# First-pass token blocks in pairs of tiles throughout, their low parts in the ring of the projection's weights

## The chip, the cores and the metric

One Trainium2 chip, one core, one launch. The metric is the device time of the whole program in microseconds (us). The kernel before was run three times: 3278.14, 3278.9 and 3288.34 us, median 3278.9.

## The reference, cut to what matters

One layer of a sequence model over 17 tiles of 128 tokens: tile 16 is the prompt (128 context tokens), tiles 0 to 15 are 2048 latent tokens. Only the first steps of the layer bear on the change:

```
h    = rmsnorm(x, norm_mix) * (1 + sc1) + sh1
proj = h @ w_in                       # 1024 -> 3088 columns
u, z_s5, qkv, z_gdn, beta, a = split(proj)
```

`u` (the first 512 columns) feeds a state-space scan over all tokens (S5), `qkv` a chunked delta-rule scan; `beta` and `a` (the last 16 columns) are its gates. An output projection, a gated residual and an MLP follow.

## The kernel before, in words

All products are made in pairs of parts: a value is split into a high part (rounded to the type that TensorE multiplies at one pass) and a low part (the rest), and a product is `wh*H + wl*H + wh*L`. So each 128x128 weight block costs three matmuls for each of the eight 128-row slices of the 1024 inputs: 24 matmuls for 128 output columns.

**First pass** (`first_cols` L258, `first_pass` L290). It goes over blocks of tiles listed in `UBLOCKS` (L221). For each tile `norm_rows` (L249) loads x, adds the position embedding (two PE products, L214 and L211, and VectorE adds, L216) and normalises the rows; `to_cols` (L162) transposes the tile in eight PE transposes (L169), applies scale and shift on VectorE (L176) and writes the high part `uH` on ScalarE (L178) and the low part `uL`, half on VectorE and half on GpSimd (L179). Both are stored to `s_hH` and `s_hL` for later groups (L280). Then for a block of n columns come four channel tiles of 24 matmuls each (L307), whose results ScalarE copies out as `eu` (L311) and SyncE stores to `s_u` (L312), and 16 narrow matmuls for the gates (L316, L318). The inputs of the next block are recorded ahead of the matmuls of this one (L296). Blocks of tiles 16 and 0 to 3 lie in one wide buffer `g0H`, `g0L` that stays for the projection; the others take `uH`, `uL` from a ring of two. Tiles 4, 5, 6 and 7 are blocks of one tile, so 128 columns wide; 8 to 15 go in pairs, 256 columns wide.

**Tables.** With the first `EARLY` blocks (L220) run the four table steps of the S5 scan (`s5_tables` L1193): products on VectorE and GpSimd (`CA`, L1028 to L1033), copies on ScalarE (L1227, L1235), small PE work (L1226, L1249), stores to `s_stab` and a last VectorE step `KK` (L1255). They share one `CA` and one `WI` buffer, so one step follows another.

**Projection of group 0** (`group_proj` L471). After the early blocks, tiles 16 and 0 to 3 are projected for channel tiles 8 to 19 (24 matmuls of 388 and 24 of 258 columns each, L482), alternating with the remaining first-pass blocks. Each of these channel tiles loads raw weights, splits them into `wh` on ScalarE (L414) and `wl` on GpSimd (L415), and stores both to `s_wc` (L398). The two parts come from pool `pw`, with two buffers of 4 KB per partition each. Later groups load `wh` and `wl` back from `s_wc` (L403): 68 times.

**What sets the order.** The program is recorded in loops that alternate generators (L1741 to L1756: three steps of the first pass and one of the tables a time); a scheduler with a timeline model then fixes the order on each engine, before the run. Engines work through their lists in order and wait on semaphores; a buffer is given out again when all who used its tile are done.

Of the kernel before, what the change touches and what calls it, by code (L numbers as in the profile page):

```python
# [9 lines left out]
FR = mybir.dt.float32r  # L10
# [150 lines left out]

def to_cols(k, h, H, L, c0, kind, r):  # L162

    nc = k.nc
    for q in range(2):
# [5 lines left out]
        for a in range(4):  # L171
# [4 lines left out]
            nc.vector.tensor_scalar(raw[:, a], pv[:, a], k.mcol[:, kind, r, i:i + 1], k.mcol[:, kind + 1, r, i:i + 1], op0=OP.mult, op1=OP.add)  # L176
        hv = H[:, 4 * q:4 * q + 4, c0:c0 + 128]
        nc.scalar.activation(hv, raw, AF.Copy)  # L178
        (nc.gpsimd if q in k.lpool and kind == 0 else nc.vector).tensor_tensor(L[:, 4 * q:4 * q + 4, c0:c0 + 128], raw, hv.bitcast(F32), op=OP.subtract)  # L179

# [36 lines left out]
    return x  # L217


EARLY = 6  # L220
UBLOCKS = ((16, 0, 1), (2, 3), (4,), (5,), (6,), (7,), (8, 9), (10, 11), (12, 13), (14, 15))  # L221


def place(t):

    if t == 16:
        return 0, 1
    return (0, 130 + 128 * t) if t < 4 else (t // 4, 1 + 128 * (t % 4))
# [20 lines left out]
def norm_rows(k, t):  # L249

    x = load_x(k, t)
    h = k.px.tile([128, 1024], F32, name="hrow")
    rs = rms_rows(k, k.psm, x, h)
    k.nc.scalar.activation(h, x, AF.Copy, scale=rs)
    return h


def first_cols(k, tiles, early):  # L258


    nc, S = k.nc, k.S
    if tiles[0] == 16 or tiles[-1] < 4:
        H, L = k.g0x
        c0s = [place(t)[1] for t in tiles]
    else:
        H = k.ph.tile([128, 8, 128 * len(tiles)], FR, name="uH")
        L = k.ph.tile([128, 8, 128 * len(tiles)], FR, name="uL")
        c0s = [128 * i for i in range(len(tiles))]
    for c, t in zip(c0s, tiles):
        h = early.pop(t) if t in early else norm_rows(k, t)  # L270
        to_cols(k, h, H, L, c, 0, int(t == 16))
    segs = [(c0s[i], t, m) for (i, t, m) in runs(tiles)]
    for part, X, X0 in (("hH", H, k.g0x[0]), ("hL", L, k.g0x[1])):
        if tiles[0] == 4:

            nc.scalar.activation(X0[:, :, 642:643], X[:, :, 0:1].bitcast(F32), AF.Copy)
        X = X.bitcast(F32)
        for (c, t, m) in segs:
            g, c0 = place(t)
            nc.sync.dma_start(S[f'{part}{g}'][:, :, c0:c0 + 128 * m], X[:, :, c:c + 128 * m])  # L280

            if t + m in (4, 8, 12):
                e = c + 128 * m
                nc.sync.dma_start(S[f'{part}{g + 1}'][:, :, 0:1], X[:, :, e - 1:e])
            if t in (8, 12):
                nc.sync.dma_start(S[f'{part}{g - 1}'][:, :, 513:514], X[:, :, c:c + 1])
    return H, L, segs


def first_pass(k, early):  # L290

    nc, S = k.nc, k.S
    cols = None
    for bi, tiles in enumerate(UBLOCKS):
        H, L, segs = cols or first_cols(k, tiles, early)

        cols = first_cols(k, UBLOCKS[bi + 1], early) if bi + 1 not in (EARLY, len(UBLOCKS)) else None
        yield None
# [93 lines left out]
def load_w(k, ct):  # L392

    nc = k.nc
    if ct not in k.wdone:
        wh, wl = split_w(k, k.I['w_in'][0][:, ct * 128:ct * 128 + 128])
        for i, w in enumerate((wh, wl)):
            nc.sync.dma_start(k.S['wc'][ct, i], w.bitcast(F32).rearrange("p k c->p (k c)"))  # L398
        k.wdone.add(ct)
        return wh, wl  # L400
    ws = [k.pw.tile([128, 8, 128], FR, name=n) for n in ("wh", "wl")]
    for i, w in enumerate(ws):
        nc.sync.dma_start(w.bitcast(F32).rearrange("p k c->p (k c)"), k.S['wc'][ct, i])  # L403
    return ws


def split_w(k, src, p=None, nm=""):
    nc = k.nc
    p = p or k.pw
    wh = p.tile([128, 8, 128], FR, name="wh" + nm)  # L410
    wl = p.tile([128, 8, 128], FR, name="wl" + nm, bufs=1 if nm else k.wlb)
    w = k.pwr.tile([128, 8, 128], F32, name="wraw")
    nc.sync.dma_start(w, src.rearrange("(k p) c->p k c", p=128))
    nc.scalar.activation(wh, w, AF.Copy)  # L414
    nc.gpsimd.tensor_tensor(wl, w, wh.bitcast(F32), op=OP.subtract)  # L415
    return wh, wl
# [1265 lines left out]
def program(tc, I, O):  # L1682
    nc = tc.nc
    k = Ctx()
# [3 lines left out]
    k.ahead = 0  # L1688
    k.acols = ()
    k.lpool = (1,)  # L1690
    k.wlb = 2
    with ExitStack() as top:
        dram = top.enter_context(tc.tile_pool(name="dram", bufs=1, space=bass.MemoryType.DRAM))
        k.S = {n: dram.tile(list(s), F32, name="s_" + n) for n, s in SHAPES.items()}
# [1 line left out]
        def pool(st, n, b, **kw):  # L1696
            return st.enter_context(tc.tile_pool(name=n, bufs=b, reuse_waits="tile", **kw))
# [4 lines left out]
        with ExitStack() as st0:  # L1702
# [12 lines left out]
            with ExitStack() as st:  # L1715
                k.psA = pool(st, "psA", 3, space=PSUM, side="right")
                for n, b in (("pa", 1), ("px", 4), ("psm", 1)):
                    setattr(k, n, pool(st, n, b, side="right"))
                k.pwr = pool(st, "pwr0", 1, side="right")
                k.peu = pool(st, "pe0", 2, side="right")  # L1720
                setup_first(k)
                params(k)
                tabs = ExitStack()
                k.psS = pool(tabs, "psS", 2, space=PSUM)
                for n in ("sa", "sb", "st"):
                    setattr(k, n, pool(tabs, n, 1))
                early = {t: norm_rows(k, t) for t in UBLOCKS[0]}
                with ExitStack() as sm:
                    k.pm = k.pmw = pool(sm, "pmw0", 5, side="right")
                    k.psM, k.mp = k.psA, "gA"  # L1730
                    m0 = modulation(k, 0)
                    advance(m0, 4)
                    s5_setup(k)
                    drain(m0)
                ab_weights(k)
                k.puw = pool(st, "puw", 1, side="right")
                u_weights(k)
                k.ph = pool(st, "ph0", 2, side="right")
                k.psu = k.psd
                first = first_pass(k, early)  # L1740
                tab = seq(*[s5_tables(k, bt) for bt in range(4)])  # L1741

                for _ in range(3 * EARLY):
                    next(first)
                    advance(tab, 1)
                drain(tab)
                tabs.close()
                k.pwr = pool(sg, "pwr1", 2)
                k.pe, k.pew = pool(sg, "pe1", 2), 388
                k.ph = pool(st, "ph0b", 2, side="right")  # L1750
                k.psu = pool(st, "psu", 2, space=PSUM, side="right")
                H, L = ([t[:, q] for q in range(8)] for t in k.g0x)
                k.cur = (H, L, [(0, 388, 385, [(0, 128, 2048), (129, 256, 0)]), (385, 258, 256, [(0, 256, 256)])], 1)
                group = group_proj(k, 0, range(8, 20))

                for i, _ in enumerate(first):  # L1756
                    advance(group, 1)
# [55 lines left out]
            with ExitStack() as st:  # L1813
# [20 lines left out]
                n = 0  # L1834
# [73 lines left out]
```

## Time and profile before

| | us |
|---|---|
| Median of three runs | 3278.9 |
| Profiled execution, its own time | 3283.95 |
| Its span | 3282.2 |
| PE busy, whole span | 3018.0 (92%) |
| DVE / POOL / ACT busy | 1986.4 / 1351.0 / 1113.0 |
| Tiles 4 to 7 (blocks of one tile) and the last tables | about 140 to 240 |
| Group 0 and the blocks of two tiles | about 240 to 405 |
| Scans, later groups | about 405 to 1620 |

PE is the array's matmul stream, PEld its weight loads (they overlap it), DVE VectorE, ACT ScalarE, POOL GpSimd, SP SyncE, which issues the DMAs. An interval written `x8` in the timeline is eight merged instructions. PEclk is the granted clock of TensorE as a share of 2.4 GHz; 0.50 is the lower of its two levels, 1.2 GHz. The DMA share is the mean busy share of 16 DMA engines; issue rows can lie a little beside the traffic they cause, so a short window can show more than 1.00.

### The profile page before, as it was taken

Reading aid. Unit: us, or ns where it says so; the run is one execution under the profiler, and the core shown is the slowest. Engines: PE = TensorE matmul, PEld = TensorE weight load, DVE = VectorE, ACT = ScalarE, POOL = GpSimd, SP = SyncE. Lnnn points to the kernel's source line nnn. Section 1 sums busy time; section 2 is a strip of 40 time slices with the busy share of each in tenths; the row PEclk is TensorE's granted clock in tenths of the full one; section 3 lists DMA queues with packets and bytes.
Section 4 is the critical chain, followed back from the end, with each engine's and each line's share of the span. In section 5 each row is a group of like instructions: output and inputs, shape, how many; then the busy total and the mean of one; then the engine's idle time right before and its main releaser. Section 6 shows DMA issues by size and latency. Waiting matters only on the chain. (4 is left out here: it accounts for less than half of the span.)

```text
span 3282.2 us, 48952 instructions
## 1 busy us (share of the span) xinstructions
PE 3018.0 (92%) x17978; PEld 2554.5 (78%) x17978; DVE 1986.4 (61%) x3842; ACT 1113.0 (34%) x2338; POOL 1351.0 (41%) x983
## 2 busy tenths in 40 slices
PE   5899989889887889988999999999999999999998
PEld 2778967677776677877888778898888887888886
DVE  6635579777776886346545368543358643684445
ACT  2334334424433222234423243322233322433332
POOL 3532223413444332246543454333444544554542
PEclk7889989898988899989999999999999999999999
DMA  7789888966567888899533455322444534553332
GB/s 208 174 178 223 237 292 259 303 220 205 176 223 228 259 277 287 299 301 321 163 95 112 150 164 167 103 77 75 134 123 143 156 97 125 164 170 100 97 96 71
DMA packets 572752, 594.98 MB, mean 181 GB/s; under 512 B 167228, under 2 KB 428592, under 8 KB 569440
## 3 DMA queue, kind: packets, MB, share of 16 engines
q1 hardware_dynamic: 572512, 591.86, 58.9%
q8 instruction: 141, 2.31, 0.3%
q14 instruction: 99, 0.81, 0.1%
HBM read 449.61 MB, written 142.13 MB: 180 GB/s over the span
## 5 line engine op out<-in xcount | busy, mean ns | idle before, releaser
L1411 POOL TENSOR_TENSOR wol<-woraw,woh 128x512 fp32r<-128x512 f32 x320 | 426.7, 1345 | 648.4 <-ACT woh L1410 637.2
L1410 ACT ACTIVATE woh<-woraw 128x512 fp32r<-128x512 f32 x320 | 193.4, 626 | 802.8 <-PE gA L1556 470.8
L1561 DVE TENSOR_TENSOR acc<-acc,gA 128x512 f32<-128x512 f32 x510 | 341.0, 682 | 192.5 <-PE gA L1556 192.4
L1556 PE MATMUL gA<-woh,ffH 128*128 128x512 f32 x1088 | 426.0, 392 | 6.8 <-ACT r L1538 3.9
L1556 PE MATMUL gA<-woh,ffL 128*128 128x512 f32 x1088 | 425.5, 391 | 1.8 <-DVE ffL L1542 1.8
L1556 PE MATMUL gA<-wol,ffH 128*128 128x512 f32 x1088 | 425.0, 391 | 0.0
L1411 POOL TENSOR_TENSOR wil<-wiraw,wih 128x1024 fp32r<-128x1024 f32 x128 | 328.6, 2569 | 112.0 <-PE gA L1534 84.7
L1541 DVE TENSOR_TENSOR r<-r 128x512 f32<-128x512 f32 (+1 forms) x160 | 163.9, 1031 | 304.7 <-ACT ffH L1540 304.4
L1534 PE MATMUL gA<-htH,wih 128*128 128x512 f32 (+1 forms) x1280 | 276.6, 362 | 5.8 <-DVE acc L1561 3.3
L1534 PE MATMUL gA<-htL,wih 128*128 128x512 f32 (+1 forms) x1280 | 272.8, 358 | 0.0
L1534 PE MATMUL gA<-htH,wil 128*128 128x512 f32 (+1 forms) x1280 | 271.9, 357 | 0.0
L1534 PEld LDWEIGHTS gA<-htH,wih 128*128 128x128 f32 x1280 | 222.8, 190 | 39.1 <-DVE acc L1561 5.0
L1534 PEld LDWEIGHTS gA<-htL,wih 128*128 128x128 f32 x1280 | 221.5, 188 | 30.6
L1556 PEld LDWEIGHTS gA<-woh,ffH 128*128 128x128 f32 x1088 | 205.4, 189 | 51.2 <-ACT r L1538 4.8
L1534 PEld LDWEIGHTS gA<-htH,wil 128*128 128x128 f32 x1280 | 220.5, 188 | 29.8
L1556 PEld LDWEIGHTS gA<-woh,ffL 128*128 128x128 f32 x1088 | 205.3, 189 | 44.0 <-DVE ffL L1542 2.2
L1556 PEld LDWEIGHTS gA<-wol,ffH 128*128 128x128 f32 x1088 | 205.3, 189 | 43.0
L482 PE MATMUL d<-hH,wh 128*128 128x258 f32 (+2 forms) x960 | 178.8, 329 | 23.1 <-DMA wh<-s_wc 18.2
L482 PE MATMUL d<-hL,wh 128*128 128x258 f32 (+2 forms) x960 | 177.8, 319 | 9.5 <-DMA hL<-s_hL 9.4
L482 PEld LDWEIGHTS d<-hH,wh 128*128 128x128 f32 x960 | 150.8, 209 | 40.6 <-issue 24.2
L482 PE MATMUL d<-hH,wl 128*128 128x258 f32 (+2 forms) x960 | 176.0, 320 | 0.0
L1410 ACT ACTIVATE wih<-wiraw 128x1024 fp32r<-128x1024 f32 x128 | 134.7, 1052 | 121.1 <-PE gA L1534 80.7
(419 smaller groups left out, 5603.0 us busy)
## 6 DMA issues: line engine op xcount, KB each, us to landing
wiraw<-in_w_mlp_in SPq DMA_DIRECT2D x128, 512.0 KB
woraw<-in_w_mlp_out SPq DMA_DIRECT2D x256, 256.0 KB
wh<-s_wc SPq DMA_DIRECT2D x68, 512.0 KB
wl<-s_wc SPq DMA_DIRECT2D x68, 512.0 KB
wada<-in_w_ada SPq DMA_DIRECT2D x24, 1024.0 KB
KVr<-s_kv SPq DMA_DIRECT2D x34, 512.0 KB
Qr<-s_qkv SPq DMA_DIRECT2D x32, 512.0 KB
woraw<-in_w_out SPq DMA_DIRECT2D x64, 256.0 KB
```

Source lines behind the costliest of these rows:

```text
L482: nc.tensor.matmul(ps[:, 0:w], W_[:, kk, :], X_[kk][:, f:f + w], start=(n == 0), stop=(n == 23))
L1410: nc.scalar.activation(h[:, i:i + n], w, AF.Copy)
L1411: sub.tensor_tensor(l[:, i:i + n], w, h[:, i:i + n].bitcast(F32), op=OP.subtract)
L1534: nc.tensor.matmul(ps[b][:, 0:w], W[:, kk, :], X[:, kk, b * w:b * w + w], start=(m == 0), stop=(m == 23))
L1541: nc.vector.tensor_tensor(r[:, 0:w], r[:, 0:w], r[:, 0:w], op=OP.mult)
L1556: nc.tensor.matmul(ps, X[:, s], W[:, hf], start=(m == 0), stop=(m == 3 * FB - 1))
L1561: nc.vector.tensor_tensor(accs[i][:, c], accs[i][:, c], ps, op=OP.add)
```

## The change

Two things. Tiles 4 to 15 all go through the first pass in pairs (five blocks, up to tile 9, stand beside the tables instead of six blocks up to tile 7). The low part of an early block no longer has a buffer of its own: it is a tile of pool `pw`, whose `wh` and `wl` become one tile `w` of two parts in a ring of two.

```
-EARLY = 6
-UBLOCKS = ((16, 0, 1), (2, 3), (4,), (5,), (6,), (7,), (8, 9), (10, 11), (12, 13), (14, 15))
+EARLY = 5
+UBLOCKS = ((16, 0, 1), (2, 3), (4, 5), (6, 7), (8, 9), (10, 11), (12, 13), (14, 15))
...
-        H = k.ph.tile([128, 8, 128 * len(tiles)], FR, name="uH")
-        L = k.ph.tile([128, 8, 128 * len(tiles)], FR, name="uL")
+        H, L = (k.uparts(n) for n in ("uH", "uL"))
...
-    ws = [k.pw.tile([128, 8, 128], FR, name=n) for n in ("wh", "wl")]
+    ws = two_parts(k)
...
+def two_parts(k):
+
+    w = k.pw.tile([128, 2, 8, 128], FR, name="w")
+    return w[:, 0], w[:, 1]
...
+                ph0 = pool(st, "ph0", 2, side="right")
+
+                k.uparts = lambda n: (ph0.tile([128, 8, 256], FR, name=n) if n == "uH" else
+                                      k.pw.tile([128, 2, 8, 128], FR, name="w").rearrange("p a k c->p (a k c)").rearrange("p (k c)->p k c", c=256))
...
+                ph0b = pool(st, "ph0b", 2, side="right")
+                k.uparts = lambda n: ph0b.tile([128, 8, 256], FR, name=n)
```

On PE, the last early block before is tile 7 alone; these are its last rows, and the first of group 0 (d are result banks, the numbered wh and wl the resident weights of the four channel tiles, uH and uL the block):

```order
L307 MATMUL d<-uH,wh_551 128x128 x8
L307 MATMUL d<-uL,wh_551 128x128 x8
L307 MATMUL d<-uH,wl_552 128x128 x8
L316 MATMUL d<-uH,ab_517 32x128 x8
L318 MATMUL d<-uL,ab_518 32x128 x8
L169 MATMUL gA<-ident,hrow 128x128 x8
L214 MATMUL gA<-posr,ident 64x512 x2
L324 MATMUL d<-ident,abT 128x32
L482 MATMUL d<-g0H,wh 128x388 x8
```

The same place on PE now (line numbers are those of the changed kernel), where the last early block is tiles 8 and 9 and its low part is a tile w:

```order
L306 MATMUL d<-uH,wh_551 128x256 x8
L306 MATMUL d<-w,wh_551 128x256 x8
L306 MATMUL d<-uH,wl_552 128x256 x8
L315 MATMUL d<-uH,ab_517 32x256 x8
L317 MATMUL d<-w,ab_518 32x256 x8
L169 MATMUL gA<-ident,hrow 128x128 x8
L214 MATMUL gA<-posr,ident 64x512 x2
L323 MATMUL d<-ident,abT 128x32 x2
L211 MATMUL gA<-cst_142,ident 128x512
L488 MATMUL d<-g0H,w 128x388 x16
```

There are as many matmuls in a block as before, each over twice the columns, and two blocks fewer in all: 960 L307 matmuls become 768. Tiles 8 and 9 have moved ahead of group 0.

On SP, the loads of stored weights in a later group, before (wh and wl are single tiles with their buffer numbers, s_wc the stored weights):

```order
L403 DMA wl_4877<-s_wc_61 128x1024
L403 DMA wh_4876<-s_wc_61 128x1024
L514 DMA s_qkv_70<-ec3_4477 128x2x128
L133 DMA wada_4434<-in_w_ada 128x2048
...
L403 DMA wl_5095<-s_wc_61 128x1024
L403 DMA wh_5094<-s_wc_61 128x1024
```

The same place on SP now:

```order
L402 DMA w_4293<-s_wc_61 128x1024 x2
L520 DMA s_qkv_70<-ec3_3646 128x128
L520 DMA s_qkv_70<-ec3_3646 128x2x128
L520 DMA s_qkv_70<-ec3_3683 128x2x128
L133 DMA wada_4144<-in_w_ada 128x2048
...
L402 DMA w_4520<-s_wc_61 128x1024 x2
```

Before, wl often stood ahead of wh, since its buffer came free first; now both parts wait for one tile and go high part first.

On PE, the end of group 0 now, where before all of it stood ahead of the first scan product (L1294, now L1300; ub and WI are the scan's inputs):

```order
L1300 MATMUL gs<-ub,WI 64x272 x4
L488 MATMUL d<-g0H,w 128x388 x16
L488 MATMUL d<-g0L,w 128x388 x3
L1300 MATMUL gs<-ub,WI 64x272 x4
L488 MATMUL d<-g0L,w 128x388 x5
```

The first-pass generator has three steps fewer after the early blocks, so three channel tiles of group 0 are left over for the loop that runs them beside the scan.

## Rows read from the trace of the kernel before

**Rows 1.** The page: busy us, share of the span, instructions

```profile
PE 3018.0 (92%) x17978; PEld 2554.5 (78%) x17978; DVE 1986.4 (61%) x3842; ACT 1113.0 (34%) x2338; POOL 1351.0 (41%) x983
```

**Rows 2.** Stretches: length, busy PE, PEld, DVE, ACT, POOL, PEclk, DMA share, GB/s

```profile
140.00:240.00 100.00, 91.85 (x691) 79.75 (x691) 36.77 (x77) 36.72 (x77) 44.38 (x33) 0.76 0.84 167
...
260.00:400.00 140.00, 136.33 (x971) 126.98 (x970) 67.69 (x147) 54.75 (x102) 35.41 (x47) 1.00 0.87 223
400.00:460.00 60.00, 45.53 (x306) 37.53 (x305) 53.80 (x162) 13.04 (x33) 10.42 (x11) 0.86 0.95 347
```

**Rows 3.** Busy time by stretches, first-pass matmuls of L307 alone

```profile
140.00:240.00 100.00, 59.17 (x384) 0.76 0.84 167
260.00:400.00 140.00, 48.51 (x376) 1.00 0.87 223
```

**Rows 4.** Timeline of PE, tile 7 alone (start, length, merged instructions)

```profile
219.93 1.11 PE L307 MATMUL d<-uH,wh 128*128 128x128 f32 x8
220.88 1.06 PE L307 MATMUL d<-uL,wh 128*128 128x128 f32 x8
```

**Rows 5.** Timeline of PE, a block of two tiles

```profile
343.97 1.12 PE L307 MATMUL d<-uH,wh 128*128 128x256 f32 x8
344.92 1.12 PE L307 MATMUL d<-uL,wh 128*128 128x256 f32 x8
```

**Rows 6.** Timeline of PE at the lower clock, 128 and 258 columns

```profile
154.80 1.91 PE L307 MATMUL d<-uL,wh 128*128 128x128 f32 x8
156.51 1.91 PE L307 MATMUL d<-uH,wl 128*128 128x128 f32 x8
...
435.79 1.92 PE L482 MATMUL d<-hH,wl 128*128 128x258 f32 x8
437.51 1.92 PE L482 MATMUL d<-hL,wh 128*128 128x258 f32 x8
```

**Rows 7.** Groups by line, gate matmuls in 140:245, then in 260:400

```profile
L316 PE MATMUL d<-uH,ab 128*32 128x128 f32 x32 | 3.0, 243 | 0.8 <-ACT eu L311 0.8
...
L316 PE MATMUL d<-uH,ab 128*32 128x256 f32 x32 | 4.4, 280 | 0.0
```

**Rows 8.** Timeline, end of the last table and start of group 0

```profile
180.47 0.17 DVE L1255 TENSOR_TENSOR KK<-KK,gs 128x16 f32<-128x16 f32 x1 [0.91 <-ACT KK L1254]
...
211.58 0.16 DVE L1255 TENSOR_TENSOR KK<-KK,gs 128x16 f32<-128x16 f32 x1
...
240.87 1.70 PE L482 MATMUL d<-g0H,wh 128*128 128x388 f32 x8
```

**Rows 9.** Timeline of PE, transposes and position products of one tile

```profile
252.89 1.03 PE L169 MATMUL gA<-ident,hrow 128*128 128x128 f32 x8
253.85 1.07 PE L214 MATMUL gA<-posr,ident 32*64 32x512 f32 x4
...
257.46 1.02 PE L211 MATMUL gA<-cst,ident 128*128 128x512 f32 x2
```

**Rows 10.** DMA queue (packets, MB, share of 16 engines): 140:260, 280:320, 440:480; issues

```profile
q1 hardware_dynamic: 44117, 21.05, 82.8%
...
q1 hardware_dynamic: 15189, 8.41, 93.4%
...
q1 hardware_dynamic: 3976, 8.70, 65.2%
...
s_u<-eu SPq DMA_DIRECT2D x16, 64.0 KB
s_hL<-uL SPq DMA_DIRECT2D x4, 512.0 KB
```

**Rows 11.** Waits in 140:245 (total us, times, longest)

```profile
POOL CA L1028 <- ACT WI L1235: 15.7, 2, 9.5
```

**Rows 12.** Waits of PE in 400:1780, and the issues of line 403

```profile
PE d L482 <- DMA wh<-s_wc: 18.2, 10, 7.7
L403 SPq DMA_DIRECT2D wl<-s_wc x68: 319/389/1875, 410.5 to 1412.3; - x68
```

More of the change, by code (lines that the diff above doesn't have):

```diff
@@ L404, in load_w @@
     return ws
+def two_parts(k):
+    w = k.pw.tile([128, 2, 8, 128], FR, name="w")
+    return w[:, 0], w[:, 1]
 def split_w(k, src, p=None, nm=""):
     nc = k.nc
-    p = p or k.pw
-    wh = p.tile([128, 8, 128], FR, name="wh" + nm)
-    wl = p.tile([128, 8, 128], FR, name="wl" + nm, bufs=1 if nm else k.wlb)
+    if p is None:
+        wh, wl = two_parts(k)
+    else:
+        wh, wl = (p.tile([128, 8, 128], FR, name=n + nm, bufs=1) for n in ("wh", "wl"))
     w = k.pwr.tile([128, 8, 128], F32, name="wraw")
@@ L1690, in program @@
     k.lpool = (1,)
-    k.wlb = 2
     with ExitStack() as top:
@@ L1737, in program @@
                 u_weights(k)
-                k.ph = pool(st, "ph0", 2, side="right")
+                ph0 = pool(st, "ph0", 2, side="right")
+                k.uparts = lambda n: (ph0.tile([128, 8, 256], FR, name=n) if n == "uH" else
+                                      k.pw.tile([128, 2, 8, 128], FR, name="w").rearrange("p a k c->p (a k c)").rearrange("p (k c)->p k c", c=256))
                 k.psu = k.psd
@@ L1749, in program @@
                 k.pe, k.pew = pool(sg, "pe1", 2), 388
-                k.ph = pool(st, "ph0b", 2, side="right")
+                ph0b = pool(st, "ph0b", 2, side="right")
+                k.uparts = lambda n: ph0b.tile([128, 8, 256], FR, name=n)
                 k.psu = pool(st, "psu", 2, space=PSUM, side="right")
```

## The prediction

> **What bounds the kernel now.** I read the page first, then the busy time by stretches, then the timeline of PE in the stretch that the change touches, then the waits and the DMA queue. On the page the reader sees PE busy 92% of the span [rows 1]: time taken from PE counts wherever PE is what the others wait for. The stretches say where that is. In 140 to 240, where tiles 4 to 7 go through the first pass one by one, PE is busy 91.85 of 100 us, at a mean granted clock of 0.76 of full; DVE, ACT and POOL are each under 45. In 260 to 400, with pairs and group 0, PE is busy 136.33 of 140 at full clock. Between 400 and 460 PE idles 14.5 of 60 us and DVE is the busiest, so what comes there depends on the scan [rows 2]. So the touched stretch is bound by PE, with the tables and the DMA (share 0.84) close behind, and the stretch after it passes any shift on.
>
> **What a block costs.** The first-pass matmuls alone show the reason for the change: 384 of them took 59.17 us for four tiles, and 376 took 48.51 us for nearly eight [rows 3]. In the timeline, groups of eight matmuls follow each other every 0.89 us over 128 columns and every 0.95 us over 256, both at full clock [rows 4, 5]. At the lower clock it is 1.71 us over 128 and 1.72 us over 258 [rows 6]. So a matmul of half the columns costs as much: 111 ns against 119, or 214 against 215.
>
> The Trainium skill (TensorE: Matmul & The Clock Gate, "Back-to-back issue gap") speaks against this in one table: 134 cycles for 128 columns and 262 for 256, warm and isolated. By it alone two pair blocks would cost what four single ones do, and the sum would be 0. The same section says that a stream of weight loads and matmuls is paced by both, so that narrow ones take longer than the table; the rows side with that sentence. I keep the table as a rival.
>
> **The sum on PE.** Removed: the four single blocks, 59.17 us [rows 3], and their gate matmuls, 3.0 us for L316 and as much taken for L318 [rows 7]: 65.2. Added: two pair blocks of 12 groups of eight, and gate matmuls of 4.4 us per four blocks and line [rows 7], so 4.4 for two blocks and both lines.
> - At full clock: 24 x 0.95 + 4.4 = 27.2, saving 38.
> - At the lower clock throughout: 24 x 1.72 = 41.3, and gates 4.4 x 1.72/0.95 = 8.0, saving 16.
> - At the clock that the stretch has now: 59.17/48 = 1.23 us per group means that (1.23 - 0.89)/(1.71 - 0.89), or 0.42 of the groups, ran low. Then a pair's group takes 0.58 x 0.95 + 0.42 x 1.72 = 1.27 us; 24 of them and gates of 5.9 make 36.4, saving 29.
>
> Nothing in the change raises the clock for certain, so PE by itself would give 29.
>
> **What comes next in line.** When PE is lighter, two other chains can end last.
>
> The tables: their last KK step ends at 211.58, 31 us after that of the table before (180.47) [rows 8]. Their steps share one buffer each, and POOL waited up to 9.5 us for ACT to free one [rows 11], so I leave their end where it is. In the new order the block of tiles 8 and 9 stands behind the last table's matmuls, with the transposes and position products of one or two tiles, about 1.0 us each and three per tile [rows 9]. The block takes 12 x 0.95 + 2.2 = 13.6 at full clock or 12 x 1.27 + 3.0 = 18.2 at the mixed one. Group 0 then starts between 211.6 + 3 + 13.6 = 228 and 211.6 + 6 + 18.2 = 236. Now it starts at 240.87 [rows 8] with tiles 8 and 9 still to do, worth 13.6 + 6 = 19.6, so the comparable moment is 260.5. Gain 24 to 32.
>
> The DMA: 82.8% of 120 us is 99.4 us of work in 140 to 260. Two stretches give the price of a packet: 15189 packets and 8.41 MB took 93.4% of 40 us on 16 engines (598 us), 3976 packets and 8.70 MB took 65.2% (417 us), so about 17 ns each beside 40 us per MB, an estimate from these two rows. The bytes stay, but 16 stores of u become eight of twice the run, 1024 runs each, and four stores each of uH and uL become two [rows 10]: 8 x 1024 + 4 x 1024 = 12288 fewer packets, 13 us of the share. That leaves 86 us; at the 93.4% that the rows reach it needs 92 us of the 120, so 28 is the most it lets through.
>
> The least of the three is at the low end of the tables' range; I take 25, near it because the clock is mixed.
>
> **Edits that I cost at nothing.**
> - Low parts in the ring of weights. Tile (4, 5) and (8, 9) share a buffer, (6, 7) has the other, so the first weights of group 0 may be split while the block (8, 9) runs, the second ones only when its matmuls and its store are done. That wait is on ACT, ahead of the last copies of `eu`, for which PE's next result banks wait. The nearest row is POOL's 9.5 us behind ACT [rows 11]; the store is issued a block earlier, so I take 0 and keep 0 to 9.5.
> - `wh` and `wl` in one tile. The low part's reload, once ahead, now waits for the last eight matmuls of its channel tile, under 1 us, while the high part no longer queues behind it. PE waited 18.2 us in all, 10 times, for the high part, in 68 loads [rows 12]. I take 0; the price is in the rivals.
> - Three channel tiles of group 0 beside the scan. They could fill part of the 14.5 idle us after 400 [rows 2], or push the scan's first copies back; between -14 and +14, taken as 0.
> - The later lists change in their interleaving only: no matmul is added or taken there.
>
> Sum: the profiled execution's own 3283.95 (span 3282.2 and 1.75 around it) - 25 = 3258.95. The median of the runs is 5.05 below the profiled one, so 3254.
>
> **Rivals.**
> - The tables or the transfers pace the early stretch (0.20). For it: DMA share 0.84 and tables ending only 29 us before group 0 [rows 2, 8]; pairs need the inputs of two tiles before their first matmul, so each table step may slip behind a longer norm chain. If each of the two last steps slips by the 9.5 us seen [rows 11], 25 - 19 = 6 is left: 3273. Against: POOL and DVE are busy under 45 of 100 us there.
> - The merged weight tile makes PE wait in later groups (0.08). Place: the start of each channel tile, L482 and its 68 loads. Price: eight matmuls, 0.95 us, for each load that now comes late. From 26 late loads on it eats the gain; if half of them, 34, and the 10 waits that exist grow by as much again, it is about 42 us: 3283.95 - 25 + 42 - 5.05 = 3296. Against: 58 of 68 loads show no wait.
> - The later stretch is dealt out anew by the scheduler and comes out some 20 us better or worse (0.08): 3234 to 3274, or beyond with a smaller gain. The idle 14.5 us in 400 to 460 show that there is something to win and lose.
> - Cost goes by columns (0.02): a pair's matmul would take twice a single's, two blocks the 65.2 us of four, and the time stays at 3279. Equal spacing at either width nearly excludes it [rows 4 to 6]. It is what the table of the Trainium skill cited above would give.
>
> **How the numbers follow.** Forecast 0.62, with its own range 3242 to 3266 (savings of 13 to 37, from the low-clock to the full-clock sum). About 0.3% (9.8 us) is what a measurement of this kernel can tell from no change. Faster: 0.62, a fifth of the first rival (0.04) and half of the third (0.04), 0.70. Slower: the second, 0.08, and a quarter of the third, 0.02, 0.10. The rest, 0.20, is no change. The range of 8 in 10 reaches from 3238 to 3278: it takes in the first rival and leaves out the second, the far ends of the third and a little of the forecast's best case.
>
> **What would show it.** Right: 256-column groups of eight every 0.95 us for tiles 4 to 7, those matmuls together some 30 us instead of 59; the first matmul of group 0 by 228 to 236 with tiles 8 and 9 done, and the end of group 0 about 25 us earlier; later stretches shifted as they are. Wrong: PE waiting longer for uH or uL or for ACT's `eu` copies in 140 to 240 with tables that end after 215; a sum of waits for s_wc well above 18 us; or a shift at 400 that is gone by 1600.

## The result, and the profile after

The changed kernel took 3244.62 us (median; 3242.63 to 3258.06) against 3283.04 us of the kernel before in the same comparison (3278.14 to 3288.34): 0.9891 of it, 95% interval 0.9858 to 0.9925. In a later comparison it was 3249.46 against 3280.29, 0.9904 (0.9886 to 0.9921). So it gained 38 and 31 us, where 25 were forecast, and it lies inside the forecast's own range. The profiled execution took 3243.24 us, its span 3241.4, 40.8 us less than the span before. How these 40.8 us are made up is another matter: the forecast put them all ahead of group 0's end, and only a part of them lies there.

The page of the changed kernel (busy us, share, instructions) answers to [rows 1]; 31.3 us less PE, nearly nothing elsewhere:

```profile
PE 2986.7 (92%) x17754; PEld 2521.9 (78%) x17754; DVE 1991.4 (61%) x3840; ACT 1112.6 (34%) x2326; POOL 1353.5 (42%) x983
```

The stretches of [rows 2] in the changed kernel (length, busy PE, PEld, DVE, ACT, POOL, granted clock, DMA share, GB/s), and in the second fence its first-pass matmuls alone (L306 now; busy PE and PEld only), as in [rows 3]:

```profile
140.00:240.00 100.00, 85.05 (x707) 70.16 (x706) 48.01 (x110) 47.99 (x89) 47.50 (x38) 0.91 0.88 224
260.00:400.00 140.00, 125.65 (x852) 116.37 (x854) 76.22 (x171) 48.80 (x93) 31.53 (x44) 0.95 0.90 262
400.00:460.00 60.00, 55.30 (x392) 44.10 (x384) 53.74 (x168) 25.80 (x78) 21.02 (x17) 0.99 0.79 266
```

```profile
140.00:240.00 100.00, 37.48 (x288) 36.23 (x288) 0.91 0.88 224
260.00:400.00 140.00, 27.18 (x216) 26.00 (x214) 0.95 0.90 262
```

In the first stretch TensorE runs at a mean clock of 0.91 instead of 0.76 and does 288 double-width matmuls in 37.48 us, where 384 single-width ones took 59.17. But in 260 to 400, which was full (136.33 of 140 at clock 1.00), PE now idles 14.4 us instead of 3.7, and its clock is 0.95. 8.8 of these 14.4 us are two waits, at 386 and at 395, for copies of projection results; the scan, which now starts at 364, has its first steps there (the first of the two waits is shown below). In 400 to 460 it is the other way: 4.7 us idle instead of 14.5.

The timeline of the changed kernel where group 0 starts, PE first, then ACT, then the last step of the tables on DVE (start, length, instructions, in brackets the idle time before and what ended it); these answer to [rows 5] and [rows 8]:

```profile
185.38 1.12 PE L306 MATMUL d<-w,wh 128*128 128x256 f32 x8
...
206.51 4.24 PE L306 MATMUL d<-uH,wh 128*128 128x256 f32 x21 [1.37 <-ACT uH L178]
...
230.42 4.60 PE L488 MATMUL d<-g0H,w 128*128 128x388 f32 x16 [5.60 <-ACT eu L310]
...
221.69 0.38 ACT L319 ACTIVATE abT<-d 32x256 f32<-32x256 f32 x1 [4.82 <-PE d L317]
226.63 1.06 ACT L420 ACTIVATE w<-wraw 128x1024 fp32r<-128x1024 f32 x1 [4.57 <-DMA x<-in_x_sample]
229.99 0.38 ACT L310 ACTIVATE eu<-d 128x256 f32<-128x256 f32 x1 [2.30 <-DMA s_u<-eu]
...
200.72 0.17 DVE L1261 TENSOR_TENSOR KK<-KK,gs 128x16 f32<-128x16 f32 x1
```

Groups of eight over 256 columns take what they took in [rows 5], every 0.95 us where they run at full clock, as forecast. Group 0 starts at 230.42, inside the forecast 228 to 236, but not by the forecast's terms: the tables end 11 us earlier than before (200.72, not 211.58), the block of tiles 8 and 9 runs from 206.5 to 221.6, and then PE waits 5.60 us for ACT. On ACT the split of the next channel tile's weights (L420) stands ahead of a copy of `eu` (L310); ACT idles 4.57 us before the split, and another 2.30 before the copy.

The end of group 0 is not the same event in the two kernels, since scan products now stand inside it. What can be compared is the moment at which two of its channel tiles are left, the blocks of the first pass are done and no scan product has run. (Three are left over in the order in which the program is recorded; on PE two stand behind the first scan product.) On PE, before and then after:

```profile
390.60 1.57 PE L482 MATMUL d<-g0H,wh 128*128 128x388 f32 x8
...
405.38 1.86 PE L1294 MATMUL gs<-ub,WI 128*64 128x272 f32 x12
```

```profile
363.98 1.14 PE L1300 MATMUL gs<-ub,WI 128*64 128x272 f32 x8
365.05 3.09 PE L488 MATMUL d<-g0H,w 128*128 128x388 f32 x16
...
386.00 3.78 PE L488 MATMUL d<-g0H,w 128*128 128x258 f32 x16 [4.60 <-DVE ec L512]
389.57 1.66 PE L488 MATMUL d<-g0L,w 128*128 128x258 f32 x8
```

That moment came at 363.98 instead of 390.60, 26.6 us earlier, and at 369.17 in the repeat of the changed kernel, 21.4 earlier. The two channel tiles that were left took 14.6 us before and 26.9 now, 12.3 more. 5.6 of these are 36 scan products, which before stood behind group 0 (PE by groups in 355 to 391):

```profile
L1300 PE MATMUL gs<-ub,WI 128*64 128x272 f32 x32 | 4.5, 405 | 0.0
L1368 PE MATMUL gs<-ub,WT 128*128 128x272 f32 x4 | 1.1, 392 | 0.0
```

4.6 are the wait at 386.00, for a copy on DVE that stands behind the first steps of the scan (L1318), which themselves waited for the scan's products:

```profile
379.87 0.63 DVE L1318 TENSOR_TENSOR Tt<-S,tb 128x272 f32<-128x272 f32 x1 [11.54 <-ACT S L1304]
...
385.24 0.61 DVE L512 SCALAR_TENSOR_TENSOR ec<-d,cw,ec 128x385 f32<-128x385 f32 x1
```

The remaining 2 us are the last matmuls, at a lower clock behind the wait: 3.78 us for 16 of 258 columns, where the tile before took 2.07.

To see where all the time went, I cut both executions at two events: the last projection matmul of group 0, and the first matmul of the output projection. Before, then after, columns as in the stretches above:

```profile
140.00:405.20 265.20, 252.80 (x1818) 229.22 (x1818) 123.77 (x267) 101.95 (x199) 85.73 (x84) 0.91 0.86 205
405.20:1438.70 1033.50, 893.35 (x7046) 754.49 (x7044) 750.10 (x1942) 353.29 (x981) 337.92 (x302) 0.91 0.78 255
1438.70:3282.20 1843.50, 1782.94 (x8588) 1513.22 (x8588) 1013.24 (x1378) 612.30 (x1085) 866.89 (x549) 0.98 0.44 136
```

```profile
140.00:390.90 250.90, 225.76 (x1671) 199.30 (x1670) 129.07 (x287) 102.54 (x190) 85.17 (x86) 0.95 0.91 243
390.90:1390.80 999.90, 887.65 (x7010) 753.26 (x7009) 755.47 (x1918) 350.54 (x973) 341.05 (x299) 0.91 0.79 256
1390.80:3241.40 1850.60, 1783.36 (x8588) 1512.93 (x8588) 1007.90 (x1378) 612.96 (x1085) 864.16 (x549) 0.98 0.44 135
```

- Early (140 to the end of group 0): 14.3 us less, with the 36 scan products (5.6 us) now inside. PE's busy time fell by 27.0, its idle time rose from 12.4 to 25.1; the waits of 5.60 and 4.60 us shown above are most of that rise.
- Middle (scans and later groups): 33.6 us less, with 36 matmuls fewer (x7046, x7010), the scan products above. For the same work it is 28.
- Late: 7.1 us more, with the same 8588 matmuls; idle 60.6 before, 67.2 after.

The forecast had 25, 0 and 0. The idle time of the middle fell by 28 us. Among PE's waits there (400 to 1440), the ones for DMA fell from 43.2 us in all to 15.1. The wait for stored weights of [rows 12] nearly went (total, times, longest):

```profile
PE d L488 <- DMA w<-s_wc: 0.4, 1, 0.4
```

Three explanations of the middle stood to be tested: the merged weights' tile (its 18.2 us of waits became 0.4), the scan that now starts inside group 0 (364 instead of 405), and a third, called theory C: the change has no part of its own in it, and the middle's length depends on how the scheduler happens to deal out the same work, by idle time and by time at the low clock.

### The profile page after: what moved, and what is told of

It reads as the page before. It is cut to its first block, busy times and chain, and to the rows that moved or that the text cites. A ratio compares the mean times of both kernels' runs of the same rounds, so it can differ in the third digit from the quotient of the medians.

```text
span 3241.4 us, 48395 instructions
## 1 busy us (share of the span) xinstructions
PE 2986.7 (92%) x17754; PEld 2521.9 (78%) x17754; DVE 1991.4 (61%) x3840; ACT 1112.6 (34%) x2326; POOL 1353.5 (42%) x983
## 2 busy tenths in 40 slices
DMA packets 560270, 594.96 MB, mean 184 GB/s; under 512 B 158844, under 2 KB 416112, under 8 KB 556960
## 5 line engine op out<-in xcount | busy, mean ns | idle before, releaser
L488 PE MATMUL d<-hH,w 128*128 128x258 f32 (+2 forms) x1920 | 335.8, 322 | 7.5 <-ACT ec L508 4.2
L488 PEld LDWEIGHTS d<-hH,w 128*128 128x128 f32 x1920 | 289.4, 203 | 34.8 <-issue 20.5
L488 PE MATMUL d<-hL,w 128*128 128x258 f32 (+2 forms) x960 | 180.8, 321 | 7.4 <-DMA hL<-s_hL 7.1
L1548 DVE TENSOR_TENSOR ffL<-r,ffH 128x512 fp32r<-128x512 f32 (+1 forms) x160 | 169.8, 1069 | 1.8
```

The costliest lines, as they stand in the source:

```text
L488: nc.tensor.matmul(ps[:, 0:w], W_[:, kk, :], X_[kk][:, f:f + w], start=(n == 0), stop=(n == 23))
L1548: nc.vector.tensor_tensor(fL[:, bs], r[:, 0:w], fH[:, bs].bitcast(F32), op=OP.subtract)
```

## The experiments

All ratios are to the kernel before, measured in the same comparison, with 95% intervals; a time is the median, a stage comes from the one profiled execution.

**Does the merged tile do it?** The kernel before with `wh` and `wl` merged into one tile, and nothing else.

```
-    ws = [k.pw.tile([128, 8, 128], FR, name=n) for n in ("wh", "wl")]
+    ws = two_parts(k)
...
+        wh, wl = two_parts(k)
```

> The kernel before with one edit: wh and wl of a channel tile lie in one tile of two parts; blocks and low parts as before. Theory A (the merged tile puts the load of the high part first and so ends PE's waits for stored weights in the later groups): the waits of PE for s_wc, 18 us before, fall under 3 us, and the time is 10 to 20 us under the kernel before. Theory B (the middle gained because three channel tiles of group 0 run beside the scan): waits may change, but the time stays within 6 us of before. Theory C (the middle's 28 us are luck of the scheduler): any shift between -15 and +15, without the waits for s_wc as its main part.

3318.21 us, 1.0112 (1.0059 to 1.0166): 35 us slower. The middle of this run, and then PE's wait for stored weights (total, times, longest):

```profile
406.60:1476.00 1069.40, 931.68 (x7047) 779.37 (x7045) 755.87 (x1942) 356.58 (x981) 346.56 (x303) 0.88 0.76 246
```

```profile
PE d L489 <- DMA w<-s_wc: 10.5, 3, 7.6
```

The wait for weights fell from 18.2 to 10.5 us, and the middle still became 35.9 us longer. Its idle time is that of before (137.7 against 140.1): what grew is the busy time of the same 7047 matmuls, by 38 us, at a clock of 0.88 instead of 0.91. So the merged tile alone is no gain, and fewer waits for stored weights did not make the middle shorter.

**The pairs without the merged tile.** The changed kernel with `wh` and `wl` in rings of their own; the low part of an early block is split into halves that lie in the two rings, and each half has stores of its own.

```
-    ws = two_parts(k)
+    ws = [k.pw.tile([128, 8, 128], FR, name=n) for n in ("wh", "wl")]
...
+class Halves:
+    def __init__(self, k):
+        self.h = [k.pw.tile([128, 4, 256], FR, name=n) for n in ("wh", "wl")]
```

> The changed kernel, but wh and wl keep their own rings of two; the low part of an early block is two halves, one in a buffer of each ring (two stores instead of one). Pairs and the order of the first pass stay. Theory A: the 20 us at the end of group 0 stay, and some 18 us of waits for stored weights come back: about 3262. Theory B: the time stays within 6 us of the changed kernel, 3245.

3278.72 us, 0.9986 (0.9964 to 1.0009): no difference to before that can be told. Its middle:

```profile
399.90:1436.80 1036.90, 905.30 (x7010) 766.70 (x7009) 762.87 (x1919) 351.69 (x973) 345.81 (x300) 0.89 0.76 247
```

The early stretch (259.9) keeps 5 us of its 14, and the first scan product comes at 373.11, 17.5 us ahead of the comparable moment before, not 26.6; the middle's 34 us are gone. Set the four kernels beside each other by their middle: single tiles and two rings 1033, single tiles and a merged tile 1069, pairs and two rings 1037, pairs and a merged tile 1000. The merged tile costs 36 us with single tiles and gains 37 with pairs; the whole times agree (35 longer, 34 shorter). But the two kernels with pairs also start the scan inside group 0 (x7010) and the two with single tiles do not, so the pairs are not the only difference between the columns. A part of a change whose effect turns its sign with another part is no term that one can add up.

**Is it the width?** The changed kernel with the channel products of tiles (4, 5) and (6, 7) done as two runs of 128 columns.

```
+            cols_ = [(0, 128), (128, 256)] if 4 <= tiles[0] < 8 else [(0, n)]
+            for (a, b) in cols_:
...
-                    nc.tensor.matmul(ps[:, 0:n], W_[:, kk, :], X_[:, kk, f:f + n], start=(m == 0), stop=(m == 23))
+                        nc.tensor.matmul(ps[:, a:b], W_[:, kk, :], X_[:, kk, f + a:f + b], start=(m == 0), stop=(m == 23))
```

> The changed kernel, with the u products of the early pairs (4,5) and (6,7) issued as two runs of 128 columns each; inputs, copies, stores and the block (8,9) stay in pairs. If the width of the matmuls is what the first 400 us gained: 192 matmuls more, 12 groups of eight at 0.89 to 1.71 us each pair, so 21 us later at full clock and up to 40 at the lower one: 3265 to 3285, and the gain at the start of group 0 is gone. If stores in fewer runs and fewer waits for the eu buffers gained it: within 8 us of the changed kernel.

3277.65 us, 0.9977 (0.9952 to 1.0002). Narrow groups of this run (L309) at the low clock and at full clock, the end of its tables, the start of its group 0, and in a fence of their own its two stages:

```profile
177.14 1.91 PE L309 MATMUL d<-uH,wl 128*128 128x128 f32 x8
...
213.43 1.05 PE L309 MATMUL d<-uH,wh 128*128 128x128 f32 x8
...
240.80 0.17 DVE L1264 TENSOR_TENSOR KK<-KK,gs 128x16 f32<-128x16 f32 x1 [0.91 <-ACT KK L1263]
...
255.55 4.67 PE L491 MATMUL d<-g0H,w 128*128 128x388 f32 x16 [3.99 <-ACT w L423]
```

```profile
140.00:419.30 279.30, 260.61 (x1883) 234.74 (x1883) 135.21 (x287) 105.68 (x196) 87.94 (x88) 0.91 0.82 219
419.30:1434.50 1015.20, 892.19 (x7011) 759.08 (x7009) 759.38 (x1920) 351.52 (x973) 340.08 (x300) 0.90 0.77 252
```

Group 0 starts 25 us later than in the changed kernel and the early stretch is 28 us longer: the width of the matmuls is what the early stretch gains from. And the tables, which the forecast took to have a pace of their own, end 40 us later (240.80 against 200.72) with no change in their own work. So they have no pace of their own. Their small matmuls stand in PE's line, which is the likely link; no run takes it apart.

**Is it the earlier scan?** The changed kernel with the rest of group 0 drained before the scan is recorded.

```
-            for _ in group:
-                scans.go()
+            drain(group)
```

> The changed kernel, but the three channel tiles of group 0 that are left over are finished before the first step of the scan, as in the kernel before. Theory B (the earlier scan makes the gain of the middle): the first scan product moves from 364 to after the end of group 0 (about 392), and the time rises by 15 to 28 us, to 3260 to 3272. Theory A: within 8 us of the changed kernel.

3248.98 us, 0.9908 (0.9881 to 0.9935). This tells less than it was meant to: the scheduler still mixed the two, and the first scan product came at 376 instead of 364. Middle 1012.9, early stretch 259.7. Counted back from the end of group 0, the scan still had a lead of 23 us, against 27 in the changed kernel, so the run does not test the early scan. The run with four early blocks, below, comes nearer to it, though it was made for another question.

**What is the wait at the start of group 0?** The changed kernel with four buffers for the first pass's results.

```
-                u = k.peu.tile([128, 8, 32], F32, name="eu")
+                u = k.peu.tile([128, 8, 32], F32, name="eu", bufs=4)
```

> The changed kernel with four instead of two buffers for the early pass's results (eu). Its ScalarE order then has all four copies of the last early block ahead of the split of channel tile 9's weights, which waits for the block's low part to be stored. Theory 1 (the 5.6 us that TensorE waits at the start of group 0 come from that split standing ahead of the copy): the wait goes, group 0 starts at 224 to 226 us instead of 230.4 and the early stretch ends about 5 us earlier. Rival 2 (the wait is for the stored rows or the weights' slot itself): group 0 still starts at 229 to 231. The whole time tells less, since the order of the middle is dealt out anew: 3225 to 3260 by the theory that the middle's length moves by some 15 us with its order, 3240 if only the 5 us count.

3237.2 us, 0.9849 (0.9829 to 0.9869). ACT and PE of this run:

```profile
218.00 0.39 ACT L310 ACTIVATE eu<-d 128x256 f32<-128x256 f32 x1 [2.66 <-PE d L306]
225.38 1.06 ACT L420 ACTIVATE w<-wraw 128x1024 fp32r<-128x1024 f32 x1 [5.12 <-DMA s_hL<-w]
...
221.89 3.10 PE L488 MATMUL d<-g0H,w 128*128 128x388 f32 x16
```

The split still waits 5.12 us, and here the releaser is named: the store of the block's low part (`s_hL<-w`) out of the same ring. But all copies of `eu` are ahead of it now, and PE goes into group 0 at 221.89 without a wait. So the wait came through ACT's list, not from the weights themselves; whether the order alone or also the 2.30 us for a free `eu` buffer made it, this run does not part. The early stretch ended 5.0 us earlier (245.9 long).

**The order of the two loads.** The changed kernel with the stored low part loaded ahead of the high part.

```
-    for i, w in enumerate(ws):
+    for i, w in reversed(list(enumerate(ws))):
```

> The changed kernel with the stored weights' low part loaded ahead of the high part. If what counts for the loads is that both parts share one tile, nothing changes that a row would show: group 0 ends at 388 to 394 us, waits for stored weights stay under 2 us, 3240 to 3255 us in all. If the order of the two loads matters (the first matmuls of a channel tile use the high part), the waits of TensorE for w grow to 5 to 15 us and the time to 3255 to 3270. A difference in the middle without such waits would speak for the theory that the middle's length depends on how the instructions happen to be dealt out.

3274.84 us, 0.9969 (0.9954 to 0.9984). Its middle, and PE's wait for stored weights:

```profile
398.20:1429.70 1031.50, 896.64 (x7008) 760.16 (x7008) 742.58 (x1918) 352.24 (x973) 342.97 (x300) 0.90 0.76 248
```

```profile
PE d L488 <- DMA w<-s_wc: 10.1, 8, 3.0
```

The waits grew from 0.4 to 10.1 us, as the second theory wanted. The middle grew by 31.6 and the early stretch by 7.3: the waits for weights are a third of the middle's part, the rest is other idle time (13 us more) and busy time (9 us more for the same matmuls, at a clock of 0.90 instead of 0.91).

**Only the middle dealt out anew, in the changed kernel.** The scan's rate is 2.5 instead of 2.

```
-            scans = Side(2, [s5_part(k, hb) for hb in range(8)])
+            scans = Side(2.5, [s5_part(k, hb) for hb in range(8)])
```

> The changed kernel with the scan dealt out beside the later groups at a rate of 2.5 instead of 2: the first-pass blocks, the tables and group 0 stay as they are up to about 391 us, the middle alone gets another order of the same matmuls. Theory C (the middle's length hangs on how the same work is dealt out, by idle time and by time at the low clock): the early stretch ends at 388 to 394 as in the changed kernel and the middle comes out anywhere between 995 and 1040 us, with a TensorE busy time that goes with its clock. Rival (the middle is set by the amount of work, and the changed kernel's 34 us there come from the pairs): the middle stays at 1000 +- 5 and the time at 3240 to 3252.

3266.2 us, 0.9936 (0.9911 to 0.996). Its middle:

```profile
392.90:1414.80 1021.90, 896.83 (x7011) 755.90 (x7010) 750.48 (x1919) 350.79 (x973) 344.84 (x300) 0.90 0.77 250
```

The early stretch (252.9) is that of the changed kernel within 2 us; in this profile the middle is 22 us longer with the same matmuls. So it lost 22 of its 34 us while the pairs, the merged tile and the early scan stayed as they are. In the whole time the two stand apart less clearly: 0.9936 against 0.9891 and 0.9904, with intervals that overlap.

**Four early blocks.** The pair (8, 9) behind the start of group 0.

```
-EARLY = 5
+EARLY = 4
```

> The changed kernel with four first blocks with the tables instead of five: the pair of tiles 8 and 9 comes behind the start of group 0, as tile 8 did in the kernel before. Theory 1 (group 0's start is set by the end of the early blocks and the tables): the tables, which end at 200.7 us in the changed kernel, are the bound, group 0 starts 15 to 25 us earlier, at 205 to 215, and the block of tiles 8 and 9 is filled in later at the same cost, so that the end of the first groups moves by less than 5 us. Rival 2 (the block is the tables' cover and nothing else has work there): TensorE idles until 215 to 230 and the time is 10 to 25 us longer. The middle's own spread of some 15 us lies on top of both: 3230 to 3275.

3260.54 us, 0.9918 (0.9893 to 0.9943). The end of the tables, and PE around it:

```profile
207.49 0.16 DVE L1261 TENSOR_TENSOR KK<-KK,gs 128x16 f32<-128x16 f32 x1
...
213.45 3.31 PE L306 MATMUL d<-uH,wh 128*128 128x256 f32 x16
...
221.73 1.68 PE L488 MATMUL d<-g0H,w 128*128 128x388 f32 x6
```

Group 0 starts at 221.73, with the block already begun, not at 205 to 215: the tables alone do not set it. The early stretch is 248.4 us long, 2.5 less than in the changed kernel, and all first-pass work still lies inside it (its last product is at 377.58).

This run also bears, by its order, on the question of the earlier scan. With three steps more of the first pass behind the tables no channel tile of group 0 is left over, and the scan starts behind all of group 0, as before. The end of group 0 and the first scan product on PE, and the middle of this run:

```profile
387.31 1.13 PE L488 MATMUL d<-g0L,w 128*128 128x258 f32 x8
388.38 1.86 PE L1300 MATMUL gs<-ub,WI 128*64 128x272 f32 x12
```

```profile
388.40:1424.50 1036.10, 913.23 (x7045) 769.16 (x7044) 743.83 (x1942) 354.24 (x980) 341.79 (x302) 0.90 0.77 254
```

Pairs and the merged tile are both there, the early scan is not, and the middle is 36 us longer than in the changed kernel, 5.6 of them the scan products, and within 3 us of the kernel before. So the earlier scan stays a rival for the gain of the middle. It is not shown either: the pair of tiles 8 and 9 moved as well, the run with two rings and the one with the low part first have the early scan and middles of 1037 and 1031, and the interval of the whole time overlaps that of the changed kernel (the late stage came out 16 us shorter).

**The control: the kernel before, its middle alone dealt out anew.** The same edit of the rate, in the kernel before.

```
-            scans = Side(2, [s5_part(k, hb) for hb in range(8)])
+            scans = Side(2.5, [s5_part(k, hb) for hb in range(8)])
```

> The kernel before with the scan dealt out at a rate of 2.5 instead of 2 and nothing else: neither pairs of tiles nor a merged weights' tile. Its instructions are the same up to the end of group 0, at 405 us, and the same work stands behind it in another order. Theory C (the middle's length hangs on the order of the same work, whatever the change): the middle, 1033 us before, moves by 10 to 40 us either way, by its idle time (140 before) and its time at the low clock (193 before), while its length without these two stays at 790 to 800. Rival (the middle's 34 us belong to the change, its pairs or its merged tile): the middle stays within 5 us of 1033 and the time within 0.3% of before.

3309.25 us, 1.0089 (1.0074 to 1.0104). Its middle:

```profile
408.30:1465.80 1057.50, 912.28 (x7044) 769.75 (x7044) 750.69 (x1941) 353.35 (x980) 339.69 (x303) 0.89 0.77 249
```

Without any part of the change the middle moves by 24 us, idle 145.2 and 235.1 at the low clock, and the whole time's interval is clear of 1. The early stretch, whose instructions are the same, differs by 3.1. That the middle moved the same way as with the changed kernel (22) leaves room for a rate that is worse in itself.

**A rate on the other side, with four buffers.** 1.75 instead of 2, against the run with four buffers.

```
-            scans = Side(2, [s5_part(k, hb) for hb in range(8)])
+            scans = Side(1.75, [s5_part(k, hb) for hb in range(8)])
```

> The changed kernel with four buffers for the early pass's results, as in the run before, and the scan at a rate of 1.75. Early stretch as there: group 0 starts at 221 to 223 and ends at 384 to 388. By theory C the middle's length without idle time and half of the time at the low clock is 790 to 800 again, and these two decide: 995 to 1040, so 3225 to 3270 in all. Rival (a slower scan is worse in itself, or better, by the rate): with 2.5 the middle was 1022, with 2 1002; by a straight line 1.75 would give 990 to 995 and 3218 to 3226.

3261.47 us, 0.9943 (0.9927 to 0.9959); early stretch 247.8, middle 1019.1, not 990 to 995. So the straight line falls. A rate of 2 was the better of three, with the changed kernel; a best rate and a chance order are not told apart by three points.

**The changed kernel and four buffers, once more and side by side.** No new edit in either.

> The changed kernel once more, on the same chip and in the same rounds as the one with four buffers, so that the two can be set against each other: 3240 to 3260, 0.9858 to 0.9925 of before.

> The changed kernel with four buffers for the early pass's results, again. If the wait at the start of group 0 is what it gains, its median lies 5 to 9 us below that of the changed kernel in the same rounds (the early stretch ended 5.0 us earlier, with the middle 2.5 us longer and the rest 8 us shorter in one profile each); if that was chance, the two medians lie within 3 us.

3249.46 us, 0.9904 (0.9886 to 0.9921), and 3245.32 us, 0.9898 (0.9883 to 0.9913). Group 0 starts at 231.72 after a wait of 6.18 us in the one and at 224.55 without a wait in the other (timeline of PE):

```profile
231.72 5.00 PE L488 MATMUL d<-g0H,w 128*128 128x388 f32 x16 [6.18 <-ACT eu L310]
```

```profile
224.55 3.10 PE L488 MATMUL d<-g0H,w 128*128 128x388 f32 x16
```

The wait is gone again, the early stretch 5.7 us shorter again; but the medians lie 4.1 us apart with overlapping intervals, and the first comparison's 0.9849 did not come again. Four buffers beat the kernel before; that they beat the changed kernel is not shown.

**All profiled executions by stage.** The low-clock time is summed over stretches of 10 us, twice (1 - granted clock) times the length of each; "rest" is the middle's length less its idle time and half its low-clock time, so roughly its work at full clock.

| kernel | early | middle | its idle | its low-clock time | its rest | late |
|---|---|---|---|---|---|---|
| before | 265.2 | 1033.5 | 140.1 | 192.9 | 797 | 1843.5 |
| before, merged tile | 266.6 | 1069.4 | 137.7 | 262.8 | 800 | 1843.9 |
| before, rate 2.5 | 268.3 | 1057.5 | 145.2 | 235.1 | 795 | 1845.4 |
| changed | 250.9 | 999.9 | 112.2 | 180.5 | 797 | 1850.6 |
| changed, again | 256.6 | 993.4 | 107.1 | 170.6 | 801 | 1848.5 |
| two rings | 259.9 | 1036.9 | 131.6 | 231.7 | 789 | 1848.0 |
| narrow matmuls | 279.3 | 1015.2 | 123.0 | 205.3 | 790 | 1840.9 |
| scan after group 0 | 259.7 | 1012.9 | 110.0 | 225.6 | 790 | 1839.8 |
| four buffers | 245.9 | 1002.4 | 116.0 | 184.6 | 794 | 1842.2 |
| four buffers, again | 250.9 | 1009.3 | 118.5 | 195.2 | 793 | 1850.4 |
| four buffers, rate 1.75 | 247.8 | 1019.1 | 117.2 | 204.7 | 800 | 1847.3 |
| high part last | 258.2 | 1031.5 | 134.8 | 208.6 | 792 | 1836.3 |
| rate 2.5 | 252.9 | 1021.9 | 125.1 | 201.4 | 796 | 1852.1 |
| four early blocks | 248.4 | 1036.1 | 122.8 | 211.6 | 808 | 1834.3 |

The rest is 789 to 808 everywhere. The first three rows and the last hold the 36 scan products (5.6 us) in their middle, the other ten ahead of it. The middle itself ranges from 993 to 1069: 1033 to 1069 in the four kernels whose scan starts behind group 0, 993 to 1037 in those whose scan starts inside it. The late stage, with the same matmuls in all, ranges from 1834 to 1852. Each row is one execution. The two kernels profiled twice came back within 7 us in the middle and 6 in the early stretch, but the 22 executions of the kernel before in one comparison spread from 3265.79 to 3302.67, so a difference of ten or fifteen us between two rows means little by itself. Kernels with nearly the same work in the middle differ by up to 76.

## Why the prediction was right early and wrong behind it

- **The sum on PE (29, by pairs at half the count): right.** First-pass matmuls in 140 to 400 fell from 108.80 us (x768) to 74.42 (x576), 34 us, against some 29 by the sum's own matmul terms. The clock's rise to 0.91, which the forecast did not count on, is the difference's likely source. The narrow run took the early gain back, so the width is the cause. The rival of a cost by columns is out. (The forecast's own range, 13 to 37, is called the low-clock to the full-clock sum; these are 16 and 38.)
- **"I leave their end where it is" (the tables): wrong.** They ended at 200.7, and at 240.8 in the narrow run. They moved with an edit of PE's matmuls alone, so they were no second bound beside PE, and the rival by which they pace the early stretch did not come.
- **The low parts in the ring, taken as 0 with 0 to 9.5 as bounds: mis-sized.** The wait came, by the path named (ACT, ahead of the last copies of `eu`), with 5.6 and 6.2 us, and went with four buffers.
- **The early 25: right in substance; "the stretch after it passes any shift on" held up to the scan.** At the start of group 0 the comparable moment came 30 us earlier (from the forecast's estimated 260.5 to 230.4), with two channel tiles left 26.6 (21.4 in the repeat). The end of group 0, by which the forecast wanted to see its 25 us, came only 14.3 earlier (8.6 in the repeat), since the early scan put 12.3 us into the last two channel tiles: 5.6 of products that no longer stand behind, the rest a wait and a lower clock.
- **Fewer packets, at most 28 from the DMA: right in number.** 572752 packets became 560270, 12482 fewer where 12288 were counted. That the DMA bounded anything early, no run shows.
- **The merged tile, 0: not a term that stands by itself.** Waits of 18.2 us became 0.4, and the rival of 34 more late loads did not come. But merged without pairs was 35 us slower.
- **Three channel tiles beside the scan, -14 to +14, taken as 0:** around the end of group 0 it comes out about even. It cost the 12.3 us above, of which 5.6 are work done ahead, and in the 60 us behind the end of group 0 PE idled 8.9 us instead of 14.5. Whether the lead of 27 us that the scan has by it shortens the rest of the middle is open.
- **"The later lists change in their interleaving only", 0: the step that failed most.** But for the 36 scan products no work left the middle, and still it fell by 33.6: 28 us of idle time, and 5.7 of busy time, which is what those products took. The forecast had this as its third rival, at 20 us either way and a chance of 0.08; the rate alone moved the kernel before by 24 us in its middle and 29 in its time, so this price was too small. That this is all that shortened the middle of the changed kernel is argued, not shown: the early scan is its rival.

So of the 40.8 us in the two profiles 26.6 came where the forecast had 25, by the cause that it named. The other 14.2 were costed at nothing and are a sum of larger terms that cancel in part: 12.3 back at the end of group 0, 33.6 gained in the middle, 7.1 lost late. That they left the time inside the forecast's range is luck. The shift was 14.3 us at the end of group 0 and 47.9 at the first product of the output projection: not gone by 1600, as the text asked, but not merely passed on either.

What stays open: which property of an order makes the middle short. Waits for weights, for DMA in all, or for the scan do not follow its length from kernel to kernel: the run with the scan after group 0 had 15.5 us of waits for weights and 41.6 for DMA in all, nearly the sums of before, and a middle of 1012.9. No run takes the early scan away and leaves all else in place, and the scan's rate was tried at three values only.

## What to carry to other kernels

Where matmuls of 128 columns cost as much as those of 256, pair them: the saving on the bound engine arrived, 27 us of it in one profile and 21 in the other. Before reading a gain off the end of a stage, look whether the next stage's work now stands inside it; here the end of group 0 made 26.6 us look like 14.3. Where a scheduler writes the order, a change early in the program can deal out anew all that follows: measure that lottery first, by an edit that changes no work (here a rate: 24 us in the kernel before), and give it a term of its own, larger than the edits one costs at nothing. And before a part of a change is called its cause, run it with and without the other part: the merged tile was worth 37 us of the middle in one company and cost 36 in the other.

## What the runs showed of the hardware that was not expected

Nearly the same matmuls (7007 to 7047) took 886 to 932 us of busy time in the middle, as the granted clock averaged 0.91 to 0.88; with a merged tile alone the idle time was unchanged and the busy time rose by 38 us. So idle time by itself does not tell how long TensorE is at its lower level: 138 us idle went with 263 us at the low clock in one order, and 140 with 193 in another. For this kernel the time at the low clock is, by this estimate, nearly as large a reserve as the idle time: half of 171 to 263 us, against 107 to 145.
